# First two feed-forward pairs side by side, all their operands through DRAM

## The chip, the cores and the metric

The kernel runs on one core of one Trainium2 chip. A core has a matrix engine (TensorE, PE in the profile; PEld is its weight load), a vector engine (VectorE, DVE), a scalar engine (ScalarE, ACT), a slower general engine (GpSimd, POOL) and a queue engine that here only issues DMA transfers (SyncE, SP). Each runs its own instructions in the order in which they were written, and they meet through semaphores. The metric is device time of one execution in microseconds (us); lower is better.

## What is computed

One encoder block in fp32 on 1024 tokens of width 1024, 8 heads, feed-forward width 2816:

```python
h = modulate(layer_norm(x), sh1, sc1)
q, k, v, u, gates = split(h @ w_in)
a_out = diff_attention(q, k, v, lam, slopes, sub_g)     # 8 heads, two softmax maps each
p_out = multiscale_pool(u, w_pool, pool_scale)
ga, gp = split(gates)
mixed = sigmoid(ga) * a_out + sigmoid(gp) * p_out
x = layer_norm(ALPHA * x + g1 * (mixed @ w_out))
h = modulate(layer_norm(x), sh2, sc2)
gt, up = split(h @ w_ffn_in)
x = layer_norm(ALPHA * x + g2 * ((silu(gt) * up) @ w_ffn_out))
```

## The kernel before, in words

**Number format.** Each fp32 operand of a matrix product is split into a high and a low part (`split`, L97: ACT casts the high part, L98, and DVE or POOL subtracts it, L99). A product is three matmuls, high by high, high by low, low by high (`mm3`, L101 to L104). A `prod` is twelve matmuls of 128x512, four slices by three.

**Heads.** The eight heads run one after another, each in eight query blocks j. A table `fill` says which other work is written behind which block: projections for the next head, the normalisation and mixing of a finished half (`rms_mix`), and in head 7 the preparation of the out-projection's weights (`wo_prep`). The functions of `fill` are written by hand; within a head the order on each engine is set by a scheduler, and the buffers by pools in which a tag has `bufs` slots. A tile waits for its slot until the last reader of the slot's tile before it is done. Raw weights of 512 KB all come into tag `raw` with three slots: the eight raw slices `wor0` to `wor7` of the out-projection, and the raw feed-forward columns `eg` (gate) and `eu` (up).

**Out-projection.** `wo_prep(k)` loads slice k, ACT casts `wo_h`, POOL subtracts `wo_l`. `out_mm(t)` multiplies token tile t: two halves of eight slices of three matmuls into PSUM `y`. Tiles 0 and 1 are done by `early` at the end of head 7. They need all eight slices, and also `mx_0h`, the mixed first half of head 7, which is made behind the row factor `rm_0f` (six small POOL operations, L684 to L690).

**Feed-forward.** It runs in 22 pairs f of 128 gate and 128 up columns, over the second half of the tokens first, by a scheme with seven instead of eight block products (Strassen and Winograd). `first_mm(f)` makes two of the products from the gate columns; five more follow with operands called 0 to 4, which are sums and differences of the weight blocks, against five token operands `t2`, `t1`, `t3`, `b22`, `t4`. The token operands are made at the transition by short DVE and ACT functions: X and X2 subtract, X2h and X2l split `t2`; D3, D3h, D3l make `t3`; B22h, B22l `b22`; X3 and X3s `t4`. `M(t)` scales token tile t on ACT out of PSUM (L465).

**Prepared ahead.** In heads 6 and 7 the generator `ffn_units` splits weights and stores them in DRAM, one unit per query block: eight gate units for pairs 0 to 3 into `wgD`, and five operand units for pair 0 into `opD`. `first_w` and `first_op` load them on POOL's queue. Operands of pairs 1 to 21 are made on the spot during the pair before (POOL `ws` L1286 and L1326, DVE L1306 and L1318, splits by `operand`).

From the transition on (`manual_schedule`) the order of all engines is the order in which the code is written.

Of the kernel before, what the change touches and what calls it, by code (L numbers as in the profile page):

```python
# [9 lines left out]
F32 = mybir.dt.float32  # L10
# [25 lines left out]
def encoder_block_kernel(  # L36
# [447 lines left out]
    with ExitStack() as ctx2:  # L484
# [231 lines left out]
        def ffn_units():  # L716


            nxt = {}
# [20 lines left out]
            yield from halves_of(0, rg)  # L740
            r11, r12, r21, r22 = block(rg, 0), block(rg, 1), block(ru, 0), block(ru, 1)
            unit(opD[4], r22, "ou4")
            yield
            pol(r22, r21, r22, op=ALU.add)
            unit(opD[1], r22, "ou1")
            yield
            pol(r21, r11, r21, op=ALU.subtract)
            unit(opD[2], r21, "ou2")
            yield
            pol(r11, r22, r11, op=ALU.subtract)  # L750
            unit(opD[0], r11, "ou0")
            yield
            pol(r12, r12, r11, op=ALU.subtract)
            unit(opD[3], r12, "ou3")
            yield

# [97 lines left out]
        for h in range(NH):  # L854
# [18 lines left out]
            else:  # L873
# [27 lines left out]
            for j in range(8):  # L901
# [57 lines left out]

    def first_w(f):  # L960
        w = (wp.tile([P, KT, P], F32R, tag="whi", bufs=2, name="wg%d_h" % f),
             wp.tile([P, KT, P], F32R, tag="wlo", bufs=2, name="wg%d_l" % f))
        for a in range(2):
            nc.gpsimd.dma_start(w[a].rearrange("p a b -> p (a b)").bitcast(F32),
                                wgD[f, a].rearrange("p h c -> p (h c)"))
        return w

    def first_op(n):

        o = (fp.tile([P, 4, P], F32R, tag="oh", bufs=4, name="oh0_%d" % n),  # L970
             fp.tile([P, 4, P], F32R, tag="ol", bufs=4, name="ol0_%d" % n))
        for a in range(2):
            nc.gpsimd.dma_start(o[a].rearrange("p a b -> p (a b)").bitcast(F32), opD[n, a])
        ops_.setdefault(0, []).append(o)

# [58 lines left out]
    def X3s(t):  # L1034
        split(*cut(t4, t), f4_[t])

    f4_ = {}
# [58 lines left out]
    with tc.manual_schedule(engines={nc.vector.engine, nc.gpsimd.engine, nc.tensor.engine, nc.scalar.engine}):  # L1096
# [4 lines left out]
        R(5); S1(5); H(2); A(5); S2(5); N(5); H(3)  # L1101
        w_[0] = first_w(0)
# [4 lines left out]
        w_[1] = first_w(1)  # L1107
        y_[7] = out_mm(7, mt[7])
# [22 lines left out]
        th_tile = lambda nm: fp.tile([P, HF], F32, tag="th", bufs=4, name=nm)  # L1131
        X2h(6)
        D3l(5); X2l(4); X2l(5); X2l(6)
        first_mm(2, w_[2])
        w_[3] = first_w(3)
        first_op(0)
        D3(7); X(7); X2(7)
        X2h(7); D3h(6); B22h(7); D3h(7)
        first_cp(2)
        X2l(7)  # L1140
        first_op(1)
        for t in range(4, 8):
            split(*cut(t1, t), hr[:, 0:4, tcol(t)])
        first_add(2, False)
        first_op(2)
        first_mm(3, w_[3])
        D3l(6); D3l(7); B22l(7)
        first_cp(3)
        first_op(3)
        X3(4); X3(5)  # L1150
# [124 lines left out]
    with tc.manual_schedule(engines={nc.vector.engine, nc.gpsimd.engine, nc.tensor.engine, nc.scalar.engine,  # L1275
                                     nc.sync.engine}):
        load_pair(1)
        load_up(1)
        for f in range(NF):
            n = f + 1  # L1280
# [6 lines left out]
            if f == 0:  # L1287
                first_op(4)
# [4 lines left out]
            if f > 0:  # L1293
                operand(f, blocks(f)[3])
            half_mul(f, 0)
            if f >= BR:
                fw_step()
            if f > 0:
                a, c11, bc = chain[f]
                c = (ps_s("fc%d" % f) if bc is None else bc)[:, HF:]  # L1300
                prod(a, ops_[f][0], t2, False, False)
                u2 = ev_tile("u2_%d" % f)
                nc.scalar.copy(u2, a)
            load_pair(f + 2)
# [3 lines left out]
            fw_store()  # L1308
            if f > 0:
                fw_step()  # L1310
            if f > 0:
                prod(c, ops_[f][1], t1, True, False)
                p5 = ev_tile("p5_%d" % f)
                nc.scalar.copy(p5, c)
            else:
                a, _, c, u2, p5 = chain[f]
            if more:
# [24 lines left out]
            fw_store()  # L1342
            fw_step()
            if f == NF - 1:
                fw_store()
                out_ops = first_out()
            half_out(f, 0, a)
            fw_store()
            if f == 0:
                hrs.close()  # L1350
                fwp = hp.enter_context(tc.tile_pool(name="fwp", bufs=1, side="right", reuse_waits="tile"))
                prep = fw_prep()
                next(prep)
    hp.close()
# [249 lines left out]
```

## Time and profile before

| what | value |
|---|---|
| three runs | 1614.96, 1617.89, 1618.81 us; median 1617.89 |
| profiled execution | 1616.56 us, of which the span from the first to the last instruction 1614.8 |
| TensorE busy | 1558.5 us, 97% of the span |
| mean granted TensorE clock | 0.991 of full speed |
| VectorE, ScalarE, GpSimd busy | 72%, 44%, 21% |

The times of a trace row are microseconds from the span's start; what the execution takes outside its span is 1.8 us. TensorE is nearly always busy, so the time can only change where TensorE waits, where its clock is lowered, or where work on it is added or removed.

### The profile page before, as it was taken

How to read it: one execution, taken by the hardware profiler on the slowest of the kernel's cores; microseconds unless marked ns; L12 is line 12 of the kernel's file. 1: busy time of each engine (PE TensorE's matmuls, PEld its weight loads, DVE VectorE, ACT ScalarE, POOL GpSimd, SP SyncE). 2: the span in 40 equal slices, each digit the busy share in tenths (PEclk: the TensorE clock that was granted, in tenths of full speed). 3: DMA queues.
4: the chain of work that ended last, by engine and by line, in shares of the span. 5: the costliest groups of instructions: out<-in, count | busy, mean ns of one | idle time of the engine just before them, and what ended most of it. 6: DMA issues, size and time to landing. Idle time of an engine off the chain costs nothing. (4 is left out here: it accounts for less than half of the span.)

```text
span 1614.8 us, 20838 instructions
## 1 busy us (share of the span) xinstructions
PE 1558.5 (97%) x7634; PEld 1299.6 (80%) x7634; DVE 1161.7 (72%) x1706; ACT 706.2 (44%) x1228; POOL 338.4 (21%) x363
## 2 busy tenths in 40 slices
PE   6899999999999999999998998999999999999996
PEld 3787888888888888888887876888888888788885
DVE  8675869597786758677674888877877888336487
ACT  4445545455454545455561244444444444323220
POOL 4300001010001211101042232433333433100013
PEclk9999999999999999999999999999999999999999
DMA  9244415142431533243526554766666665996673
GB/s 332 63 114 143 141 60 150 59 135 75 114 115 52 157 111 98 78 144 119 170 72 192 175 187 145 258 220 212 233 228 235 208 228 183 373 388 212 201 274 127
DMA packets 191448, 273.90 MB, mean 170 GB/s; under 512 B 10161, under 2 KB 126962, under 8 KB 191346
## 3 DMA queue, kind: packets, MB, share of 16 engines
q1 hardware_dynamic: 183984, 251.04, 47.1%
q0 software_dynamic: 4400, 16.25, 2.7%
q10 hardware_dynamic: 2962, 5.27, 1.0%
q8 instruction: 60, 0.98, 0.3%
q14 instruction: 42, 0.34, 0.1%
HBM read 180.26 MB, written 83.89 MB: 164 GB/s over the span
## 5 line engine op out<-in xcount | busy, mean ns | idle before, releaser
L640 ACT ACTIVATE e<-e,nm 128x1024 f32<-128x1024 f32 x128 | 147.1, 1151 | 108.4 <-DVE nm L638 107.1
L638 DVE CUSTOM_DVE_ANT_0 e<-s,table 128x1024 f32<-128x1024 f32 x128 | 153.1, 1217 | 21.7 <-PE s L633 21.2
L631 PE MATMUL s<-k,q 128*128 128x512 f32 x256 | 105.2, 411 | 1.2 <-DVE nm L638 1.2
L99 DVE TENSOR_TENSOR al<-at,ah 128x512 fp32r<-128x512 f32 x128 | 83.2, 684 | 29.1 <-ACT ah L98 28.5
L633 PE MATMUL s<-k,q 128*128 128x512 f32 x256 | 101.6, 397 | 0.0
L645 DVE SCALAR_TENSOR_TENSOR e<-e,c,e 128x1024 f32<-128x1024 f32 x64 | 87.3, 1364 | 1.8
L98 ACT CAST oh<-ws 128x512 fp32r<-128x512 f32 x84 | 51.7, 616 | 83.3 <-POOL ws L1326 45.2
L98 ACT CAST ah<-at 128x512 fp32r<-128x512 f32 x128 | 70.0, 596 | 40.5 <-PE at L654 40.5
L99 DVE TENSOR_TENSOR ol<-ws,oh 128x512 fp32r<-128x512 f32 x84 | 70.4, 839 | 19.0 <-ACT oh L98 18.9
L99 DVE TENSOR_TENSOR fw<-fw,fw 128x512 fp32r<-128x512 f32 x77 | 80.1, 1040 | 0.0
L1326 POOL TENSOR_TENSOR ws<-rg,ru 128x512 f32<-128x512 f32 x21 | 44.4, 2112 | 152.2 <-DVE ol L99 152.2
L654 PE MATMUL at<-ident,e 128*128 128x128 f32 x512 | 68.9, 275 | 5.5 <-DVE e L645 3.2
L102 PE MATMUL av<-ah,vh 128*128 128x256 f32 x256 | 73.8, 288 | 0.3 <-ACT ah L98 0.2
L104 PE MATMUL av<-ah,vl 128*128 128x256 f32 x256 | 72.5, 283 | 0.0
L103 PE MATMUL av<-al,vh 128*128 128x256 f32 x256 | 72.4, 283 | 0.0
L104 PE MATMUL oa<-w,mol 128*128 128x512 f32 x176 | 68.6, 390 | 1.2 <-DVE mol L99 1.2
L102 PE MATMUL oa<-w,moh 128*128 128x512 f32 x176 | 68.6, 390 | 0.0
L103 PE MATMUL oa<-w,moh 128*128 128x512 f32 x176 | 68.5, 389 | 0.0
L102 PE MATMUL fa<-oA,oh 128*128 128x512 f32 x176 | 68.5, 389 | 0.0
L103 PE MATMUL fa<-oA,oh 128*128 128x512 f32 x176 | 68.5, 389 | 0.0
L104 PE MATMUL fa<-oA,ol 128*128 128x512 f32 x176 | 68.5, 389 | 0.0
L654 PEld LDWEIGHTS at<-ident,e 128*128 128x128 f32 x512 | 58.8, 144 | 11.2 <-DVE e L645 3.6
(578 smaller groups left out, 4608.1 us busy)
## 6 DMA issues: line engine op xcount, KB each, us to landing
wfD<-fw SPq DMA_DIRECT2D x77, 512.0 KB, 3.5
w<-wfD SPq DMA_DIRECT2D x77, 512.0 KB, 4.3
ada<-in_w_ada_dram SPq DMA_DIRECT2D x32, 512.0 KB, 3.8
fw<-in_w_ffn_out_dram SPq DMA_DIRECT2D x44, 256.0 KB, 4.4
rg<-in_w_ffn_in_dram SPq DMA_DIRECT2D x21, 512.0 KB, 4.2
ru<-in_w_ffn_in_dram SPq DMA_DIRECT2D x21, 512.0 KB, 3.8
midD<-th SPq DMA_DIRECT2D x42, 256.0 KB, 2.2
q<-q SPq DMA_DIRECT2D x32, 256.0 KB, 2.9
```

The source lines that it names most:

```text
L98: nc.scalar.copy(hi, src)
L99: (eng or nc.vector).tensor_tensor(lo, src, hi.bitcast(F32), op=ALU.subtract)
L102: nc.tensor.matmul(ps, lh, rh, start=start, stop=False, skip_group_check=skip)
L103: nc.tensor.matmul(ps, lh, rl, start=False, stop=False, skip_group_check=skip)
L104: nc.tensor.matmul(ps, ll, rh, start=False, stop=stop, skip_group_check=skip)
L631: nc.tensor.matmul(ps[:, cs], q[:, 0, jj * P:(jj + 1) * P], kd[h, m][:, cs], start=True, stop=False)
L633: nc.tensor.matmul(ps[:, cs], q[:, 1, jj * P:(jj + 1) * P], kd[h, m][:, cs], start=False, stop=True)
L638: nc.vector.tensor_tensor_reduce(out=t, in0=ps, in1=table[:, o0:o0 + S], scale=-slope, scalar=3.0e38, op0=ALU.add, op1=ALU.min, accum_out=nm)
L640: nc.scalar.activation(t, t, AF.Exp, bias=nm, scale=-1.0, accum_out=zt[:, m, j:j + 1])
L645: nc.vector.scalar_tensor_tensor(s[1], s[1], c1, s[0], op0=ALU.mult, op1=ALU.add)
L654: nc.tensor.matmul(pt[:, i, :], a[:, kt * P:(kt + 1) * P], ident, start=True, stop=True, is_transpose=True)
L1326: pol(sa, blocks(n)[0], blocks(n)[2], op=ALU.subtract)
```

## The change

All seven products' operands of pair 1 are made in the attention phase too, as those of pair 0 were. The gate units move from heads 6 and 7 to heads 4 and 5, and the ten operand units run in head 7 (one or two per query block, from j = 1). For pair 1 this brings two raw loads (`eg1`, `eu1`), five splits and four POOL additions or subtractions (L741 to L750 after) into head 7. In head 7 the second part of the mixing of the first half moves one place up. At the transition `first_w(2)` and `first_w(3)` are issued on ACT's queue, ahead of `M(7)`; X2h(6) goes ahead of `M(7)`; `t1` is made earlier and D3h(6), D3h(7) and B22h(7) later. The products of pairs 0 and 1 are written out alternately, and pair 2's operands are made during them. The arithmetic is the same.

```diff
-    opD = dram.tile([5, 2, P, HF], F32, tag="opD", name="opD")
+    opD = dram.tile([2, 5, 2, P, HF], F32, tag="opD", name="opD")
...
-                t = at.tile([P, 2, HF], F32R, tag="acc", name=nm)
+                t = at.tile([P, 2, HF], F32R, tag="mh" if nm[0] == "w" or nm[-1] in "13" else "acc", name=nm)
...
-            for f in (1, 2, 3):
+            for f in (3, 2, 1, 0):
                 yield from halves_of(f, gcols(f))
-            rg, ru = gcols(0), load_raw(wcols(wfi, DFF), "eu0")
...
+            for f in (0, 1):
+                rg, ru = gcols(f), load_raw(wcols(wfi, DFF + f * P), "eu%d" % f)
+                r11, r12, r21, r22 = block(rg, 0), block(rg, 1), block(ru, 0), block(ru, 1)
+                unit(opD[f, 4], r22, "ou%d_4" % f)
+                pol(r22, r21, r22, op=ALU.add)
+                yield
+                unit(opD[f, 1], r22, "ou%d_1" % f)
+                pol(r21, r11, r21, op=ALU.subtract)
+                yield
+                unit(opD[f, 2], r21, "ou%d_2" % f)
+                pol(r11, r22, r11, op=ALU.subtract)
+                yield
+                unit(opD[f, 0], r11, "ou%d_0" % f)
+                pol(r12, r12, r11, op=ALU.subtract)
+                yield
+                unit(opD[f, 3], r12, "ou%d_3" % f)
+                yield
...
-                    6: [lambda: wo_prep(4), lambda: wo_prep(5), lambda: wo_prep(6), lambda: wo_prep(7)],
-                    7: [lambda: rms_mix(h, 0, 1), lambda: early(0), lambda: early(1)],
+                    6: [lambda: wo_prep(4), lambda: wo_prep(5), lambda: wo_prep(6), lambda: wo_prep(7),
+                        lambda: rms_mix(h, 0, 1)],
+                    7: [lambda: early(0), lambda: early(1)],
...
-                elif h >= 6 and (h, j) > (6, 0):
-                    next(units, None)
+                elif h in (4, 5) and j % 4 == 3:
+                    next(units)
+                    next(units)
+                elif last and j > 0:
+                    for _ in range(1 + (2 < j < 6)):
+                        next(units, None)
...
         first_add(0, False); N(7); T(7)
+        w_[2] = first_w(2, nc.scalar)
         first_cp(1)
+        w_[3] = first_w(3, nc.scalar)
...
-        X2h(5)
+        X2h(5); X2h(6)
         M(7)
-        w_[2] = first_w(2)
...
-        for f in range(NF):
+        half_gate(0, 0, chain[0][1])
+        for n in range(2):
+            first_op(1, n)
+        a, _, c, u2, p5 = chain[0]
+        prod(a, ops_[0][2], t3, False, False)
...
+        prod(c, ops_[0][3], b22, False, True)
...
+        rest_a(1)
...
+        prod(a1, ops_[1][2], t3, False, False)
...
+        prod(c1, ops_[1][3], b22, False, True)
...
+        pair_ops(2, 0)
+        prod(a, ops_[0][4], t4, False, True)
+        pair_ops(2, 1)
...
+        prod(a1, ops_[1][4], t4, False, True)
...
+        pair_ops(2, 3)
+        for f in range(2, NF):
```

`rest_a(f)` holds the two products with operands 0 and 1 (`t2`, `t1`). `pair_ops(2, step)` is new and makes pair 2's operands in four steps: step 0 is the POOL addition `ws`, a DVE subtraction and a split.

On POOL, at the end of head 7, before the change, from the last two operations of `rm_0f` on:

```order
L95 TENSOR_TENSOR rm_0f<-rm_0v,mhalf 128x4
L690 TENSOR_TENSOR rm_0f<-rm_0f,rm_0m 128x4
L99 TENSOR_TENSOR wo_l<-wor_7547,wo_h 128x1024
L99 TENSOR_TENSOR wo_l<-wor_7551,wo_h 128x1024
L99 TENSOR_TENSOR wo_l<-wor_7555,wo_h 128x1024
L682 TENSOR_TENSOR rm_1z<-zt_6952 128x4
L683 TENSOR_SCALAR rm_1v<-rm_1z 128x4
L686 TENSOR_SCALAR rm_1z<-rm_1z 128x4
L99 TENSOR_TENSOR wo_l<-wor_7559,wo_h 128x1024
```

The same place after it:

```order
L95 TENSOR_TENSOR rm_0f<-rm_0v,mhalf 128x4
L690 TENSOR_TENSOR rm_0f<-rm_0f,rm_0m 128x4
L741 TENSOR_TENSOR eu_7422<-eu_7422 128x512
L744 TENSOR_TENSOR eu_7422<-eg_7420,eu_7422 128x512
L747 TENSOR_TENSOR eg_7420<-eu_7422,eg_7420 128x512
L750 TENSOR_TENSOR eg_7420<-eg_7420 128x512
L99 TENSOR_TENSOR wo_l<-wor_7514,wo_h 128x1024
L682 TENSOR_TENSOR rm_1z<-zt_6962 128x4
L683 TENSOR_SCALAR rm_1v<-rm_1z 128x4
L686 TENSOR_SCALAR rm_1z<-rm_1z 128x4
L99 TENSOR_TENSOR wo_l<-wor_7518,wo_h 128x1024
L99 TENSOR_TENSOR wo_l<-wor_7568,wo_h 128x1024
```

Before, four of the eight `wo_l` stood ahead of these rows and four are left; after, two stand ahead, then come the four operations of pair 1 (`eu`, `eg`), and six `wo_l` are left.

On SP, in head 7, before the change (`wor` are the raw slices of the out-projection):

```order
L793 DMA wor_7502<-woD 128x1024
L793 DMA wor_7547<-woD 128x1024
L793 DMA wor_7551<-woD 128x1024
L793 DMA wor_7555<-woD 128x1024
L793 DMA wor_7559<-woD 128x1024
```

After it, the part from the second raw slice on:

```order
L791 DMA wor_7412<-woD 128x1024
L108 DMA eg_7420<-in_w_ffn_in_dram 128x8x128
L108 DMA eu_7422<-in_w_ffn_in_dram 128x8x128
L725 DMA opD<-ou_3_7416 128x2x512
L791 DMA wor_7514<-woD 128x1024
L725 DMA opD<-ou_4_7424 128x2x512
L725 DMA opD<-ou_1_7522 128x2x512
L791 DMA wor_7518<-woD 128x1024
L725 DMA opD<-ou_2_7527 128x2x512
L791 DMA wor_7568<-woD 128x1024
L798 DMA mt_0_7798<-mixD 128x7x128
L791 DMA wor_7572<-woD 128x1024
```

The raw columns of pair 1 now take slots of tag `raw` between the second and the third slice. `eg_7420` keeps its slot until the last operand unit is split, behind all slices, so that slices 2 to 7 go through two slots.

On ACT, at the transition, before the change (L1079 is X2h, L1067 B22h, the row of L465 is `M(7)`):

```order
L1079 CAST oA<-hr 128x4x128
L986 COPY p_1_8559<-fa_8521 128x512
L1067 CAST oB<-hr 128x4x128
L1079 CAST oA<-hr 128x4x128
L465 ACTIVATE hr<-m_7t,modc 128x128 x8
L1079 CAST oA<-hr 128x4x128
L1079 CAST oA<-t2s 128x4x128
```

After it (L1089 is X2h, L1077 B22h, L967 `first_w`):

```order
L1089 CAST oA<-hr 128x4x128
L967 DMA wg_h<-wgD 128x1024
L967 DMA wg_l<-wgD 128x1024
L989 COPY p_1_8593<-fa_8551 128x512
L967 DMA wg_h<-wgD 128x1024
L967 DMA wg_l<-wgD 128x1024
L1077 CAST oB<-hr 128x4x128
L1089 CAST oA<-hr 128x4x128 x2
L465 ACTIVATE hr<-m_7t,modc 128x128 x8
```

The two pairs of weight loads stand on ACT ahead of `M(7)`, and X2h of tile 6 stands ahead of it too.

## Rows read from the trace of the kernel before

**Rows 1.** The page: busy time of the engines, and one group of instructions.

```profile
PE 1558.5 (97%) x7634; PEld 1299.6 (80%) x7634; DVE 1161.7 (72%) x1706; ACT 706.2 (44%) x1228; POOL 338.4 (21%) x363
...
L645 DVE SCALAR_TENSOR_TENSOR e<-e,c,e 128x1024 f32<-128x1024 f32 x64 | 87.3, 1364 | 1.8
```

**Rows 2.** Waits of TensorE, 840 to 1045 us: total, times, longest.

```profile
PE fa L102 <- issue: 6.1, 1, 6.1
PE at L654 <- DVE e L645: 3.2, 1, 3.2
PE y L102 <- ACT mx_0h L98: 2.4, 1, 2.4
PE fa L102 <- DMA wg_h<-wgD: 2.0, 1, 2.0
...
PE fa L104 <- DMA wg_l<-wgD: 0.5, 1, 0.5
```

**Rows 3.** Timeline of TensorE, out-projection: start, duration.

```profile
876.94 0.48 PE L102 MATMUL y<-wo_h,mt 128*128 128x512 f32 x1
877.42 0.39 PE L102 MATMUL av<-ah,vh 128*128 128x256 f32 x1
...
881.63 0.28 PE L104 MATMUL av<-ah,vl 128*128 128x256 f32 x1
```

**Rows 4.** Timeline of POOL, end of head 7.

```profile
832.03 10.51 POOL L99 TENSOR_TENSOR wo_l<-wor,wo_h 128x1024 fp32r<-128x1024 f32 x4 [16.79 <-ACT wo_h L98]
842.50 0.20 POOL L684 TENSOR_TENSOR rm_0v<-rm_0s,rm_0v 128x4 f32<-128x4 f32 x1
...
844.60 8.05 POOL L99 TENSOR_TENSOR wo_l<-wor,wo_h 128x1024 fp32r<-128x1024 f32 x3
...
854.37 2.40 POOL L99 TENSOR_TENSOR wo_l<-wor,wo_h 128x1024 fp32r<-128x1024 f32 x1
```

**Rows 5.** The tile wor, all eight: duration ns min/median/max, and landing.

```profile
L98 ACT CAST wo_h<-wor x8: 1049/1052/1070, 830.9 to 850.4; 128x1024 fp32r<-128x1024 f32 x8
L99 POOL TENSOR_TENSOR wo_l<-wor,wo_h x8: 2348/2406/3408, 832.0 to 854.4; 128x1024 fp32r<-128x1024 f32 x8
...
DMA to landing us min/median/max: 3.2/3.4/6.8
```

**Rows 6.** DMA issues, 740 to 870 us: KB each, median us to landing.

```profile
eu<-in_w_ffn_in_dram SPq DMA_DIRECT2D x1, 512.0 KB, 4.2
```

**Rows 7.** POOL by form, 980 to 1500 us: busy us, mean ns.

```profile
L1326 POOL TENSOR_TENSOR ws<-rg,ru 128x512 f32<-128x512 f32 x21 | 44.4, 2112 | 152.2 <-DVE ol L99 152.2
L1286 POOL TENSOR_TENSOR ws<-ru 128x512 f32<-128x512 f32 x21 | 32.8, 1560 | 54.3 <-DMA ru<-in_w_ffn_in_dram 36.6 <-ACT u L1090 9.5 <-DVE th L1261 3.8
```

**Rows 8.** Timeline of TensorE, transition to the feed-forward.

```profile
969.53 0.47 PE L102 MATMUL fa<-h0h,wg_h 128*128 128x512 f32 x1 [2.02 <-DMA wg_h<-wgD]
...
981.29 0.39 PE L102 MATMUL fa<-oA,oh 128*128 128x512 f32 x1
981.52 0.39 PE L103 MATMUL fa<-oA,oh 128*128 128x512 f32 x1
...
998.75 0.76 PE L102 MATMUL fa<-oB,oh 128*128 128x512 f32 x1 [6.07 <-issue]
```

**Rows 9.** A stretch: busy us (instructions) by engine, granted clock, DMA share, GB/s.

```profile
1000.00:1020.00 20.00, 20.00 (x84) 16.35 (x84) 14.46 (x21) 9.26 (x17) 7.43 (x6) 0.93 0.64 207
```

**Rows 10.** Timeline of DVE: head 7, and the transition.

```profile
847.32 3.07 DVE L645 SCALAR_TENSOR_TENSOR e<-e,c,e 128x1024 f32<-128x1024 f32 x1
...
971.90 0.69 DVE L1076 TENSOR_TENSOR hr<-hr 128x512 f32<-128x512 f32 x1
...
997.97 0.68 DVE L1323 TENSOR_TENSOR p<-p,fa 128x512 f32<-128x512 f32 x1
```

**Rows 11.** Timeline of ACT, transition.

```profile
969.17 2.90 ACT L465 ACTIVATE hr<-m_7t,modc 128x128 f32<-128x128 f32 x8
972.63 0.62 ACT L1079 CAST oA<-hr 128x512 fp32r<-128x512 f32 x1 [0.56 <-DVE hr L1076]
```

More of the change, by code (lines that the diff above doesn't have):

```diff
@@ L963, in first_w, with first_op @@
         for a in range(2):
[L964 to L971 removed]
+            q.dma_start(w[a].rearrange("p a b -> p (a b)").bitcast(F32),
+                        wgD[f, a].rearrange("p h c -> p (h c)"))
+        return w
+    def first_op(f, n):
+        o = (fp.tile([P, 4, P], F32R, tag="oh", bufs=4, name="oh%d_%d" % (f, n)),
+             fp.tile([P, 4, P], F32R, tag="ol", bufs=4, name="ol%d_%d" % (f, n)))
         for a in range(2):
[L973 to L974 removed]
+            nc.gpsimd.dma_start(o[a].rearrange("p a b -> p (a b)").bitcast(F32), opD[f, n, a])
+        ops_.setdefault(f, []).append(o)
     def first_mm(f, w):
@@ L1035, in X3s, with T1l, T1 @@
         split(*cut(t4, t), f4_[t])
+    def T1l(t):
+        o = cut(t1, t)
+        vec(o[1], hr[:, 0:4, tcol(t)], o[0].bitcast(F32), op=ALU.subtract)
+    def T1(t):
+        split(*cut(t1, t), hr[:, 0:4, tcol(t)])
     f4_ = {}
@@ L1131, in encoder_block_kernel @@
         th_tile = lambda nm: fp.tile([P, HF], F32, tag="th", bufs=4, name=nm)
-        X2h(6)
         D3l(5); X2l(4); X2l(5); X2l(6)
         first_mm(2, w_[2])
-        w_[3] = first_w(3)
-        first_op(0)
+        first_op(0, 0)
         D3(7); X(7); X2(7)
-        X2h(7); D3h(6); B22h(7); D3h(7)
+        T1(4)
+        nc.scalar.copy(cut(t1, 5)[0], hr[:, 0:4, tcol(5)])
+        X2h(7); X2l(7)
+        first_op(0, 1)
+        nc.scalar.copy(cut(t1, 6)[0], hr[:, 0:4, tcol(6)])
+        nc.scalar.copy(cut(t1, 7)[0], hr[:, 0:4, tcol(7)])
         first_cp(2)
[L1140 to L1143, printed above, removed]
+        T1l(5)
         first_add(2, False)
-        first_op(2)
+        T1l(6); T1l(7)
+        D3h(6); B22h(7); D3h(7)
+        first_op(0, 2)
         first_mm(3, w_[3])
@@ L1148, in encoder_block_kernel @@
         first_cp(3)
-        first_op(3)
+        first_op(0, 3)
         X3(4); X3(5)
@@ L1276, in encoder_block_kernel, with pair_ops @@
                                      nc.sync.engine}):
-        load_pair(1)
-        load_up(1)
-        for f in range(NF):
+        load_pair(2)
+        load_up(2)
+        load_pair(3)
+        def pair_ops(n, step):
+            w11, w12, w21, w22 = blocks(n)
+            if step == 0:
+                ops_[n, "s"] = [evp.tile([P, 4, P], F32, tag="st", bufs=2, name="ws%d_%d" % (n, i)) for i in range(2)]
+            sa, sb = ops_[n, "s"]
+            if step == 0:
+                pol(sa, w21, w22, op=ALU.add)
+                vec(sb, sa, w11, op=ALU.subtract)
+                operand(n, sb)
+            elif step == 1:
+                vec(sb, w12, sb, op=ALU.subtract)
+                operand(n, sa)
+                pol(sa, w11, w21, op=ALU.subtract)
+            elif step == 2:
+                operand(n, sa)
+            else:
+                operand(n, sb)
+        half_gate(0, 0, chain[0][1])
[3 more added lines that the diff above has]
+        prod(a, ops_[0][2], t3, False, False)
+        vec(p5, p5, a, op=ALU.add)
+        half_mul(0, 0)
+        first_op(1, 2)
+        prod(c, ops_[0][3], b22, False, True)
+        vec(u2, u2, c, op=ALU.add)
+        half_gate(0, 1, u2)
+        first_op(1, 3)
+        rest_a(1)
+        hrs.close()
+        fwp = hp.enter_context(tc.tile_pool(name="fwp", bufs=1, side="right", reuse_waits="tile"))
+        prep = fw_prep()
+        next(prep)
+        first_op(0, 4)
+        a1, _, c1, u21, p51 = chain[1]
+        first_op(1, 4)
+        prod(a1, ops_[1][2], t3, False, False)
+        half_mul(0, 1)
+        vec(p51, p51, a1, op=ALU.add)
+        half_out(0, 1, p5)
+        prod(c1, ops_[1][3], b22, False, True)
+        vec(u21, u21, c1, op=ALU.add)
+        half_gate(1, 0, chain[1][1])
+        half_mul(1, 0)
+        pair_ops(2, 0)
+        prod(a, ops_[0][4], t4, False, True)
+        pair_ops(2, 1)
+        half_gate(1, 1, u21)
+        pair_ops(2, 2)
+        load_up(3)
+        half_out(0, 0, a)
+        prod(a1, ops_[1][4], t4, False, True)
+        half_mul(1, 1)
+        half_out(1, 1, p51)
+        half_out(1, 0, a1)
+        pair_ops(2, 3)
+        for f in range(2, NF):
             n = f + 1
@@ L1292, in encoder_block_kernel @@
             half_gate(f, 0, chain[f][1])
-            if f > 0:
-                operand(f, blocks(f)[3])
+            operand(f, blocks(f)[3])
             half_mul(f, 0)
-            if f >= BR:
+            if f > 2:
                 fw_step()
[L1298 to L1303, printed above, removed]
+            a, c11, bc = chain[f]
+            c = (ps_s("fc%d" % f) if bc is None else bc)[:, HF:]
+            prod(a, ops_[f][0], t2, False, False)
+            u2 = ev_tile("u2_%d" % f)
+            nc.scalar.copy(u2, a)
             load_pair(f + 2)
@@ L1308, in encoder_block_kernel @@
             fw_store()
[L1309 to L1316, printed above, removed]
+            fw_step()
+            prod(c, ops_[f][1], t1, True, False)
+            p5 = ev_tile("p5_%d" % f)
+            nc.scalar.copy(p5, c)
             if more:
@@ L1343, in encoder_block_kernel @@
             fw_step()
+            if f == 3:
+                fw_step()
             if f == NF - 1:
@@ L1348, in encoder_block_kernel @@
             fw_store()
[L1349 to L1353, printed above, removed]
     hp.close()
```

25 lines of the change are left out of this document (3 added, 22 removed).

## The prediction

> **What bounds the kernel now.** I read the page first: TensorE is busy 97% of the span, VectorE 72% and ScalarE 44% [rows 1]. So only TensorE's own idle time and its clock can be won or lost. Next the waits of TensorE, limited to the two places that the change touches. Five matter there [rows 2]. At the end of head 7 it waits 3.2 us for the softmax tile `e` and 2.4 us for `mx_0h`. At the transition it waits 2.0 and 0.5 us for the weights of `first_mm(2)`, and 6.1 us ahead of one matmul of a product. The profile calls the last one "issue", so I looked at VectorE's timeline beside it: the product starts at 998.75 [rows 8] just after the DVE addition `p<-p,fa`, which reads the PSUM tile that it overwrites, has ended at 997.97 + 0.68 = 998.65 [rows 10]. That addition is queued behind the splits of `t4` and those of pair 1's operands. The reader should see that this wait belongs to VectorE's backlog. Last, the clock: the stretch from 1000 us has 0.93 with TensorE fully busy [rows 9], so 14% of its 20 us, 2.8 us, went at the lower level, 1.2 instead of 2.4 GHz. With the part from 998.75 on that is 4.05 us in which half the work was done, a loss of 2.0 us.
>
> **Part one, the transition: a gain.** What can be won is 2.0 + 0.5 + 6.1 us of waits and 2.0 us of clock, 10.6 us. Step by step:
>
> Weights of pairs 2 and 3 are issued earlier, on a queue where nothing is waiting. `first_mm(2)` then starts at 969.53 - 2.02 = 967.5 [rows 8]. One matmul takes 0.227 us (981.29 to 981.52 [rows 8], rounded there), a `prod` of twelve 2.72. After three products, at 975.7, `first_mm(3)` needs the PSUM tile that `M(7)` empties. `M(7)` now stands behind X2h(6). Its source X2(6) ends at 971.90 + 0.69 = 972.59 [rows 10], the cast takes 0.62 and `M(7)` 2.90 [rows 11], so it ends at 976.2 where it ended at 972.07. The wait is 0.5 us. Behind `M(7)` stand X(7), X2(7), X2h(7) and X2l(7), in sum four DVE operations of 0.69 and one cast of 0.62: 3.4 us, with hand-overs near 4, so `t2` is whole at about 980.2. `first_mm(3)` is through at 978.9 and `rest_a(0)` starts at 980.2 instead of 981.29 [rows 8]. Of 2.5 us, 1.1 are won.
>
> The 6.1 us wait: four products (10.9 us) now stand between the product with `b22` and the one with `t4` of pair 0, and VectorE is rid of five splits and two subtractions of pair 1, 7 x 0.69 = 4.8 us. Either covers the backlog. I count the 6.1 and the 2.0 us of clock as won, 8.1.
>
> Pair 2's operands are the next that can be late. From `pair_ops(2, 0)` two products, 5.4 us, pass before the first is used; it needs a POOL addition (1.56 to 2.11 us, [rows 7]), two DVE operations (1.38) and a cast (0.62): 3.6 to 4.1 us with nothing in the way, but `half_gate`, `half_mul` and `half_out` of two pairs share DVE and ACT. If they fit, it costs 0.3; if four of those 0.69 us operations stand ahead it costs 2.9. I take 1.6. The operand loads of pair 1 cost nothing: eight products lie between the first issue and the last use. If that cover were gone, a late load would cost up to its landing.
>
> Gain of this part: 1.1 + 8.1 - 1.6 = 7.6 us, from 6.3 to 8.9.
>
> **Part two, the end of head 7: a loss.** Before, POOL made the eight `wo_l` between 832.03 and 856.77, only interrupted by `rm_0f` and three small operations [rows 4]; three raw slots let each load run under the subtractions. TensorE reached tile 2 at 876.94 [rows 3]. After the change four POOL operations and two loads stand between the second and third slice, and slices 2 to 7 use two slots, since `eg1` holds the third. The chain:
>
> 1. The first two `wo_l` at 10.51/4 = 2.63 us each: 832.0 + 5.3 = 837.3 [rows 4].
> 2. `eu1` takes the slot that the second leaves, 4.2 us [rows 6]: 841.5.
> 3. ACT casts it (0.62) ahead of the copy that `rm_0f` needs, together 0.8: 842.3. Then `rm_0f`, 844.60 - 842.50 = 2.1 [rows 4]: 844.4. TensorE waits here for `mx_0f`, which moved up.
> 4. Four POOL operations of 128x512. The rows have means of 1.56 and 2.11 [rows 7]; I take the middle, 1.84, as both rows have the same shape: 7.4, 851.8. The third `wo_l` 2.63: 854.4.
> 5. The fourth slice's load waits for the third's slot, the sixth's for the fourth's and the eighth's for the sixth's. Each round is a load 3.4, a cast 1.05 [rows 5], `wo_l` 2.63 and 0.1 between: 7.2. Three rounds: 876.0.
> 6. In the order, 52 matmuls of tiles 0 and 1 stand behind the first that needs the eighth `wo_l`: 11.8 us. Tile 2 starts at 887.8, 10.9 later than before.
> 7. Before, the 24 `av` matmuls of the last block (0.12 us each, 2.9) and the `ms` and transposes about them (1.2) ran after the start of tile 2 [rows 3]; now they run in the waits. That gives back 4.1. The longer waits bring one more stretch of lowered clock, priced as the one above, 2.0 at most; I take 1.8.
>
> Loss: 10.9 - 4.1 + 1.8 = 8.6 us. Lower bound: POOL operations of 1.56, loads of 3.2, `wo_l` of 2.35 [rows 5] and no clock loss: rounds of 6.7, the eighth ends at 873.1, loss 3.9. Upper bound: 2.11, one load of 6.8 [rows 5]: 880.5, loss 13.1.
>
> A row shows POOL and VectorE in each other's way: while `wo_l` ran, L645 took 3.07 us [rows 10], where its group's mean is 1.36 [rows 1]. The Trainium skill has a rule for it ("SBUF — State Buffer", section "SBUF: two separate sides"): the port pair that GpSimd and VectorE share is an exclusive lock, so that a VectorE operation with two SBUF inputs waits until a GpSimd operation that holds it is done. By that rule four more POOL operations block VectorE up to four times; the row agrees. What this makes of the time is the fourth rival.
>
> **The rest.** The gate units in heads 4 and 5 add eight pairs of a cast (0.62) and a DVE split (0.69) there and take them out of heads 6 and 7. VectorE and ScalarE have room [rows 1]; with no cover they would cost 10.5 us, but then their leaving heads 6 and 7 would win as much. I count 0, as I do for `t1` and D3h, B22h, which only change places within the cover of `first_mm`.
>
> **Sum.** 1616.56 (the profiled execution, span 1614.8) + 8.6 - 7.6 = 1617.6. The three runs have a median 1.3 above that execution, so the median forecast is 1618.9, put down as 1619: no change that can be told. A measurement of this kernel can tell about 0.3%, 4.9 us. Its own range goes from 3.9 - 8.9 = -5.0 to 13.1 - 6.3 = +6.8: 1613 to 1625.
>
> **Rivals.**
> 1. *Slower: loads on the two slots decide.* Rounds in step 5 run beside the `mt` loads and `opD` stores that now stand between them on SP. If two of the three loads take the longest landing, 6.8 [rows 5], the sum rises by 6.8: 1626. For it: SP issues in order, and a slice's load stands behind stores that wait for splits. Against it: 3.4 is the median of eight. It decides once the eighth `wo_l` ends after about 880.
> 2. *Faster: the chain is covered.* If the eighth `wo_l` ended by 869 (rounds of 5 us, or loads that come earlier), tile 2 would start near 881, its 4.1 us are given back, and the loss is about 0 to 1: 1618 - 7 = 1611. For it: TensorE has `av`, transposes and the first slices of two tiles to do in between. Against it: a round's three durations alone are 7.1.
> 3. *The change doesn't do what it says.* If pair 2's operands or `M(7)` give back most of the transition, the gain is 3 instead of 7.6: 1623.5. For it: the operand chain has under 2 us to spare.
> 4. *VectorE is blocked in head 7.* Four POOL operations of 1.84 keep it from the splits and `e` tiles that `at` and `mx_0h` wait for; half of their 7.4 us would reach TensorE: 1622.7. Against it: TensorE is waiting for `wo_l` there anyway.
>
> **Chances.** My forecast 0.50, the rivals 0.20, 0.17, 0.06 and 0.07. Faster by over 0.3%: rival 2 and a little of the forecast's lower end, 0.19. Slower: rival 1, half of 3 and 4, and the upper end of the forecast, 0.31. Within: 0.50. The range that leaves out no more than 2 in 10 reaches from rival 2's value to just beyond rival 1's: 1611 to 1627; outside stay loads slower still, and a chain wholly covered.
>
> **What the profile will show.** Right: no wait of over 1 us at the product with `t4` of pair 0, tile 2 starting near 888, the eighth `wo_l` ending near 876, waits of TensorE on POOL's `rm_0f` and `wo_l` in head 7. Wrong: if the `wo_l` end before 869 or the loads land in far over 3.4; if `rest_a(0)` starts later than 981 relative to `m_7t`; or if TensorE waits over 3 us for pair 2's operands.

## The result, and the profile after

The changed kernel takes 1626.81 us (median of four runs, 1626.48 to 1627.85) against 1616.91 for the kernel before on the same chip: a ratio of 1.0062, 95% interval 1.0045 to 1.008. It is slower by 10 us, 0.6%, which is clear of noise. The time lies within the range that was given, near its upper end. It lies 1.8 us above the forecast's own range (1613 to 1625), and the likeliest case, no change, was not what came.

The waits of TensorE after the change, from 840 to 1060 us and from 1060 us on (total, times, longest), answer to [rows 2]. They are quoted from two answers of the same view.

```profile
PE mx_0f L190 <- POOL rm_0f L690: 5.2, 1, 5.2
PE y L103 <- POOL wo_l L99: 4.0, 4, 1.3
PE fc L102 <- ACT p L1383: 3.3, 2, 2.7
PE fa L102 <- ACT p L989: 2.5, 1, 2.5
PE y L102 <- ACT wo_h L98: 1.7, 2, 0.9
PE fa L104 <- DMA wg_l<-wgD: 1.1, 1, 1.1
...
PE ob L102 <- DMA w<-wfD: 3.8, 1, 3.8
```

Of the five waits that the prediction started from, four are gone or at most 0.5 us. The fifth, on `wg_l`, grew from 0.5 to 1.1 us. Six others stand beside it, and only the first, the second and the fifth row are those of head 7 that were foreseen. The two rows `fc` and `fa ... p` are in pairs 2 to 4, and the last one is where the output stage begins, 350 us later.

To see what each is worth I took the starts of the same matmuls from the timelines of both traces. Two rows of the changed kernel and two of the kernel before stand for the method:

```profile
961.00 0.30 PE L460 MATMUL m_6t<-ident,m_6n 128*128 128x128 f32 x1
...
1013.98 0.39 PE L102 MATMUL fa<-oA,oh 128*128 128x512 f32 x1
```

```profile
954.51 0.30 PE L460 MATMUL m_6t<-ident,m_6n 128*128 128x128 f32 x1
...
1017.02 0.39 PE L102 MATMUL fa<-oA,oh 128*128 128x512 f32 x1
```

At `m_6t` the changed kernel is 6.5 us behind; at the first product of pair 2 it is 3.0 us ahead; and it ends 9.9 behind. The stages between such marks, in us:

| from | to | before | after | difference |
|---|---|---|---|---|
| first `wo_l` | `m_6t` | 122.48 | 129.24 | +6.8 |
| `m_6t` | pair 0, product with `t2` | 26.78 | 25.15 | -1.6 |
| there | pair 2, first product | 35.73 | 27.84 | -7.9 |
| there | pair 4, first product | 27.77 | 32.75 | +5.0 |
| there | pair 5, first product | 19.04 | 21.89 | +2.9 |
| there | pair 21, first product | 304.64 | 305.03 | +0.4 |
| there | end | 246.34 | 251.05 | +4.7 |

With the first `wo_l` 0.3 us earlier (831.76 against 832.03) the sum is +10.0, the difference of the spans is 1624.7 - 1614.8 = 9.9.

POOL's timeline at the end of head 7, after the change, answers to [rows 4]:

```profile
831.76 5.23 POOL L99 TENSOR_TENSOR wo_l<-wor,wo_h 128x1024 fp32r<-128x1024 f32 x2 [16.79 <-ACT wo_h L98]
...
844.51 1.26 POOL L741 TENSOR_TENSOR eu<-eu 128x512 f32<-128x512 f32 x1
...
850.17 2.41 POOL L99 TENSOR_TENSOR wo_l<-wor,wo_h 128x1024 fp32r<-128x1024 f32 x1
...
857.73 2.37 POOL L99 TENSOR_TENSOR wo_l<-wor,wo_h 128x1024 fp32r<-128x1024 f32 x1 [3.92 <-ACT wo_h L98]
...
864.95 2.46 POOL L99 TENSOR_TENSOR wo_l<-wor,wo_h 128x1024 fp32r<-128x1024 f32 x1 [1.53 <-ACT wo_h L98]
...
873.62 2.35 POOL L99 TENSOR_TENSOR wo_l<-wor,wo_h 128x1024 fp32r<-128x1024 f32 x1 [3.46 <-ACT wo_h L98]
```

From the first to the last `wo_l` it takes 44.2 us where it took 24.7. The reader should see POOL idle ahead of the last slices: it waits for the cast, the cast for the load, and the load for the slot.

### The profile page after: what moved, and what is told of

Read it like the earlier page. It is cut to its first block, busy times and chain, and to the rows that moved or that the text cites. A ratio compares the mean times of both kernels' runs of the same rounds, so it can differ in the third digit from the quotient of the medians.

```text
span 1624.7 us, 20878 instructions
## 1 busy us (share of the span) xinstructions
PE 1560.1 (96%) x7634; PEld 1300.8 (80%) x7634; DVE 1162.2 (72%) x1704; ACT 704.2 (43%) x1228; POOL 341.0 (21%) x371
```

## The experiments

Each kernel is compared with the kernel before in runs on the same chip. The changed kernel's ratio is 1.0062. Profiles of kernels with the same code up to there differ in when the first `wo_l` starts (831.76 in the changed kernel, 833.81 in the first experiment), so stages are compared from mark to mark.

Stages of the same code differ between profiles too, and a difference has to be larger than that. The changed kernel and those of experiments 1, 3 and 4 have the same code up to `m_6t`: their eight `wo_l` take 44.2, 46.0, 46.5 and 45.5 us, and `m_6t` comes 129.2, 130.2, 130.2 and 129.4 us after the first. Experiments 2, 5, 6 and 11 have the changed kernel's code from `m_6t` on: from pair 2 to pair 4 they take 31.2, 32.7, 31.2 and 31.6 us, and for the last stage 249.8, 249.2, 249.7 and 249.3, where the changed kernel takes 32.75 and 251.05.

**1. Head 7 alone.** The attention phase of the changed kernel with everything from `first_w` on of the kernel before:

```diff
-            nc.gpsimd.dma_start(o[a].rearrange("p a b -> p (a b)").bitcast(F32), opD[n, a])
+            nc.gpsimd.dma_start(o[a].rearrange("p a b -> p (a b)").bitcast(F32), opD[0, n, a])
```

> The attention phase of the changed kernel (gate units in heads 4 and 5, ten operand units in head 7, mixing moved up) with the transition and the feed-forward of the kernel before; pair 1's operands are stored and not used, the result is the same. Theory A (the chain through POOL and two raw slots in head 7 costs 6 to 7 us by itself, whatever follows): eighth wo_l ends near 876, m_6t starts 6.5 us later than before, total 6 to 7 us above the kernel before, about 1623. Rival B (what head 7 loses is covered again by the 6.1 us wait ahead of the t4 product, since VectorE works off its backlog in the meantime): the t4 wait shrinks and the total is within 2 us of the kernel before, about 1618.

Measured: 1625.54 us, ratio 1.0051 (1.0037 to 1.0064); the medians alone, against 1615.54, give 1.0062. From the first `wo_l` to `m_6t` 130.22 us, 7.7 more than before; the stages behind pair 2's first product are those of the kernel before to 0.02 us. From `m_7t` to the product with `t2` it takes 1.5 us longer. The waits for the weights are as before (1.9 and 0.5 us), but eight matmuls behind them take over 0.6 us instead of 0.39, the lower clock level (the granted clock from 978 to 985 us is 0.76). The wait ahead of the `t4` product is shorter (5.0 us instead of 6.1), and that stage with its clock takes 1.9 us less. Theory A holds: these two nearly cancel, and the loss of head 7 is not covered again.

**2. The units spread over heads 6 and 7.**

```diff
-                elif last and j > 0:
-                    for _ in range(1 + (2 < j < 6)):
-                        next(units, None)
+                elif h >= 6 and (h, j) > (6, 0):
+                    next(units, None)
```

> The changed kernel with its ten operand units spread one per query block over heads 6 and 7 (seven in head 6, three at the start of head 7), so that both raw loads and the four POOL operations of pair 1 are done before the first wo_l. Theory A: the eighth wo_l ends near 857 again, TensorE's waits on rm_0f and wo_l in head 7 (9 us) fall to those of the kernel before, m_6t starts 6 to 7 us earlier than in the changed kernel, total about 1620. Rival B (the late waits on operands and weights in the feed-forward set the time, and an earlier start only makes them longer): total 1625 to 1627. Rival C (the units cost as much in head 6): m_6t moves by under 3 us.

Measured: 1619.47 us, ratio 1.0021 (1.0013 to 1.003), so 0.41% is won back. The eight `wo_l` take 25.6 us, and from the first to `m_6t` it is 120.97 us, 8.3 less than in the changed kernel (6 to 7 expected) and 1.5 less than before the change. Theory A holds, though not in the wait on `rm_0f`: it is still 5.2 us, yet costs nothing that `m_6t` shows. What stays above the kernel before is the loss behind pair 2 (31.15 and 23.48 us instead of 27.77 and 19.04) and in the last stage (249.84).

**3. Pair 2's operands earlier.**

```diff
+        pair_ops(2, 0)
         vec(u21, u21, c1, op=ALU.add)
+        pair_ops(2, 1)
         half_gate(1, 0, chain[1][1])
         half_mul(1, 0)
-        pair_ops(2, 0)
         prod(a, ops_[0][4], t4, False, True)
-        pair_ops(2, 1)
```

> The changed kernel with pair 2's operand steps 0 and 1 written ahead of the half gates of pair 1, so that POOL's second addition is done some 2 to 3 us earlier and the raw slot for pair 3's up columns comes free earlier. Theory A (the 2.7 us wait ahead of pair 2's b22 product, with a stretch of lowered clock behind it, comes from the load of pair 3's up columns being issued late): the load is issued near 1012 instead of 1014.8, the wait goes, total 3 to 5 us below the changed kernel, about 1623. Rival B (that wait is VectorE's backlog of gate halves): the wait stays at 2 us or more, total within 1.5 us of the changed kernel.

Measured: 1622.14 us, ratio 1.0038 (1.0023 to 1.0052). The load of `ru` of pair 3 is issued 1.0 us ahead of pair 2's first product instead of 0.8 behind it, 1.8 us earlier. The wait ahead of pair 2's `b22` product, from TensorE's timeline of this kernel:

```profile
1025.33 0.50 PE L102 MATMUL fc<-oB,oh 128*128 128x512 f32 x1 [0.94 <-ACT p L1383]
```

In the changed kernel it was 2.73 us, so it fell by 1.8 too, with the load. From pair 2 to pair 4 it takes 29.40 us instead of 32.75. Theory A holds; the load moved less than I had expected, and 0.9 us stays. In the total it is less sure: the interval overlaps that of the changed kernel, and 1.6 us of the gain lie in the last stage (249.4 us), where the code is the same.

**4. The preparation steps.** `fw_step` prepares one of the 77 output weight tiles and `fw_store` issues its store.

```diff
+        fw_step()
         pair_ops(2, 2)
         load_up(3)
...
         half_out(1, 0, a1)
+        fw_store()
+        fw_step()
         pair_ops(2, 3)
+        fw_store()
...
-            if f == 3:
-                fw_step()
```

> The changed kernel with the two extra steps of the output weights' preparation put into the part where pairs 0 and 1 run side by side, and none extra in pair 3, so that all 77 are done by the end of pair 20 as before. Theory A (the 77th step falling into the last pair delays the last store and with it the first loads of the output stage; the second step in pair 3 makes ACT wait for a store): the 3.8 us wait on the weights at the start of the output stage goes down to under 1, the 2.5 us wait at the start of pair 4 goes, total 5 to 8 us below the changed kernel, about 1620. Rival B (the wait at the output stage comes from the last halves' stores, not from the weights' steps): it stays, total 2 to 3 us below.

Measured: 1620.24 us, ratio 1.0026 (1.0016 to 1.0035). From pair 4 to pair 5 it is 19.04 us again and the last stage 246.05, both as before the change. The first loads of the output stage are issued on SP in the changed kernel (`w<-wfD`), behind the last stores (`wfD<-fw`):

```profile
1376.13 0.38 SPq L1217 DMA_DIRECT2D wfD<-fw  x1
...
1377.93 6.75 SPq L1217 DMA_DIRECT2D wfD<-fw  x2
1384.81 1.18 SPq L1181 DMA_DIRECT2D w<-wfD  x2
```

and in this one, which is 1.6 us earlier at pair 21:

```profile
1376.26 0.39 SPq L1217 DMA_DIRECT2D wfD<-fw  x1
1377.46 1.05 SPq L1181 DMA_DIRECT2D w<-wfD  x2
```

One store fewer stands ahead. The loads go out 7.4 us earlier, 5.8 counted from pair 21. Theory A holds. The wait of pair 2 on `p` grows to 3.8 us (33.20 us from pair 2 to pair 4). I put this down to the two steps, which now run on ACT and DVE there; experiment 12 bears it out.

**5. The slots.** The last four units at block 5:

```diff
-                elif last and j > 0:
-                    for _ in range(1 + (2 < j < 6)):
+                elif last and 0 < j < 6:
+                    for _ in range((0, 1, 1, 2, 2, 4)[j]):
```

> The changed kernel with only the count of units per block in head 7 altered: the last four operand units of pair 1 run at block 5 instead of 5 to 7, so that pair 1's raw gate columns give back their slot before the sixth slice and the later slices use three slots. The four POOL operations stay. Theory A1 (two slots make most of the loss: three round trips of about 7 us): the eighth wo_l ends 4 to 7 us earlier than in the changed kernel, counted from the first, total 3 to 5 us lower, about 1623. Theory A2 (the POOL operations make it): it ends within 2 us of the changed kernel, total 1625 to 1627.

Measured: 1625.53 us, ratio 1.0057 (1.0041 to 1.0073), not told apart from the changed kernel. The last three `wo_l` now run back to back, but the eight take 42.0 us, 2.2 less than in the changed kernel and no more than the spread of 44.2 to 46.5. A1 alone, with 4 to 7, is wrong. The fourth slice's load still waits here until the third `wo_l` ends, so not every round trip is gone.

**6. Without POOL's operations for pair 1.**

```diff
-                pol(r22, r21, r22, op=ALU.add)
+                if f == 0:
+                    pol(r22, r21, r22, op=ALU.add)
```

and so for the other three.

> The changed kernel without the four POOL additions and subtractions of pair 1; so pair 1's operands 0 to 3 hold plain blocks and pair 1's products are not those of the reference. Loads, casts, splits, stores and slots are the same. Theory A2 (POOL's extra 5.7 us are passed on whole): the eighth wo_l ends 5 to 6 us earlier, total 4 to 6 us lower than the changed kernel, about 1622. Theory A1 (the slot round trips set the end): under 3 us earlier in the chain, total 0 to 3 us lower.

Measured: 1622.84 us, ratio 1.0042 (1.0028 to 1.0057). The eight `wo_l` take 42.2 us, 2.0 less, and to `m_6t` it is 128.39, 0.9 less than in the changed kernel, both about the spread. So A2, with 5 to 6 us, is wrong too in the chain. The total's interval overlaps that of the changed kernel. Where the profile is shorter, it is so in later stages: from pair 2 to pair 5 52.1 us instead of 54.6, and the last 249.66 instead of 251.05. The code there is the same, and why they differ stays open.

**7. The three corrections together** (experiments 2, 3 and 4 in one).

> The changed kernel with the three corrections together: operand units spread over heads 6 and 7, pair 2's operand steps earlier, the two preparation steps moved ahead of pair 2. Theory A (the three losses are separate): the differences to the changed kernel add up, 7 + 4.7 + 6.6 us, total about 1609, 6 to 8 us below the kernel before, which is what the transition wins. Rival B (what one correction wins runs into the next late operand): total 1613 to 1617, no better than the kernel before.

Measured: 1610.63 us (1607.76 to 1611.78), ratio 0.9967 (0.9955 to 0.9979): faster than the kernel before by 5.4 us. The three gains in ratio, 0.41%, 0.24% and 0.36%, sum to 1.01%; together they are 0.95%. Theory A holds, though 5.4 us is a little under the 6 to 8 expected. Its waits from 600 us on:

```profile
PE mx_0f L190 <- POOL rm_0f L690: 5.2, 1, 5.2
PE fc L102 <- ACT p L1386: 1.8, 1, 1.8
PE fa L102 <- ACT u L1377: 1.5, 1, 1.5
```

**8. The mixing back at its old place**, on top of experiment 7.

```diff
-                        lambda: rms_mix(h, 0, 1)],
-                    7: [lambda: early(0), lambda: early(1)],
+                    7: [lambda: rms_mix(h, 0, 1), lambda: early(0), lambda: early(1)],
```

> As the kernel with the three corrections, and the second part of head 7's mixing back at its old place. Theory A (TensorE's wait of 5.2 us on rm_0f in head 7 stands there because its four matmuls were moved up; back at the old place the same work fills it): that wait goes, those on e and mx_0h of the kernel before (3.2 and 2.4 us) come back, total within 1 us of the kernel with the three corrections. Rival B (moving it up costs by itself): total 2 to 4 us lower.

Measured: 1611.61 us, ratio 0.9972 (0.9962 to 0.9983), not told apart from experiment 7. The 5.2 us wait is replaced by 3.2 on `e` and 0.8 on `mx_0h`. From the first `wo_l` to `m_6t` it is 121.62 instead of 120.67: Theory A holds.

**9 and 10. The weights of pairs 2 and 3 on POOL's queue at their old places**, on top of experiment 7; in experiment 10 also X2h(6) behind `M(7)`.

```diff
         M(7)
+        w_[2] = first_w(2, nc.gpsimd)
...
-        X2h(5); X2h(6)
+        X2h(5)
         M(7)
+        X2h(6)
```

> The kernel with the three corrections, with the weights of pairs 2 and 3 loaded on POOL's queue at their old places behind M(7) again. Theory A (the early load on ACT wins the 2.5 us waits of first_mm(2), of which 1 to 2 us reach the end): TensorE waits about 2 us again on the weights, total 1 to 2.5 us above the kernel with the three corrections, about 1612. Rival B (the next waits, for t2 and for pair 2's operands, take it over): within 1 us.

> The kernel with the three corrections, with both the old places of those weight loads and X2h of tile 6 behind M(7) again. Theory A (putting X2h ahead of M(7) costs 0.5 us at PSUM and about 1 us at t2): 0.5 to 1.5 us below the kernel with only the old loads, M(7) ending 0.6 us earlier. Rival B (its place does nothing, since the weights come later than M(7) ends): no difference to it.

Measured: 1611.11 us (ratio 0.9969, 0.9957 to 0.998) and 1611.78 (0.9974, 0.9963 to 0.9984). In both TensorE waits 1.9 us for the weights again, and from `m_7t` to the product with `t2` it takes 14.73 and 14.75 us instead of 13.33; to pair 2's first product it is then 27.20 instead of 27.93. So 1.4 us are lost and 0.7 come back, which the totals can't tell from nothing (Rival B of experiment 9). X2h's place alone changes nothing here (Rival B of experiment 10).

**11. Experiments 5 and 6 together.**

> The changed kernel without pair 1's four POOL operations and with its last four units at block 5, so that the slot comes back early; pair 1's operands 0 to 3 hold plain blocks, so its products are not those of the reference. Theory A3 (POOL's operations and the slots cover each other: each alone hides behind the other): from the first to the last wo_l it takes 36 us or less where the changed kernel takes 44.2, and the total is near 1619. Rival B (the load of pair 1's up columns ahead of the row factor, and the order on ACT and SP that the units bring, set the chain): it takes 40 us or more, total 1622 to 1625.

Measured: 1623.34 us, ratio 1.0042 (1.0027 to 1.0056), which again overlaps the changed kernel's; the profiled execution took 1618.77 us. The eight `wo_l` take 39.4 us, 4.8 less than in the changed kernel (6 to 7 less than in the three others of its code), and `m_6t` is 3.9 us earlier where the parts gave 1.0 and 0.9. That hints that each partly hid behind the other; the spread of 1.0 us leaves it unsure. But 14.7 us of the 19.5 that the change added stay. The rows of POOL show where, and below them one of ACT and one of SP:

```profile
832.36 5.22 POOL L99 TENSOR_TENSOR wo_l<-wor,wo_h 128x1024 fp32r<-128x1024 f32 x2 [16.79 <-ACT wo_h L98]
846.59 2.39 POOL L99 TENSOR_TENSOR wo_l<-wor,wo_h 128x1024 fp32r<-128x1024 f32 x1 [1.42 <-ACT wo_h L98]
855.68 6.75 POOL L99 TENSOR_TENSOR wo_l<-wor,wo_h 128x1024 fp32r<-128x1024 f32 x2 [2.89 <-ACT wo_h L98]
864.69 7.09 POOL L99 TENSOR_TENSOR wo_l<-wor,wo_h 128x1024 fp32r<-128x1024 f32 x3 [2.27 <-ACT wo_h L98]
```

```profile
841.81 0.62 ACT L98 CAST ou<-eu 128x512 fp32r<-128x512 f32 x1 [4.29 <-DMA eu<-in_w_ffn_in_dram]
```

```profile
849.01 0.33 SPq L795 DMA_DIRECT2D wor<-woD  x1
```

There are 9 us between the second and the third, and 6.7 to the fourth, each up to a cast on ACT. In the first gap ACT stands 4.29 us for the load of `eu1`, ahead of the copy that `rm_0f` needs, as steps 2 and 3 of the prediction had it. In the second the load of the fourth slice is issued at 849.01, just when the third `wo_l` ends (846.59 + 2.39 = 848.98), so this slice still waits for a slot: the units at block 5 free one only for later slices. Rival B is nearer. How those us divide between the load of `eu1`, the slots, ACT's order and SP's order I did not separate; that they come with the units in head 7 is what experiment 2 shows.

**12. The extra steps later.** Experiments 2 and 3, and the extra steps in pairs 8 and 14:

```diff
-            if f == 3:
+            if f in (8, 14):
                 fw_step()
```

> The units spread over heads 6 and 7 and pair 2's operand steps earlier, as in the kernel with the three corrections, but the two extra preparation steps put into pairs 8 and 14 instead of the part where pairs 0 and 1 run side by side. Theory A (the 3.3 us that pairs 2 and 3 still lose in the kernel with the three corrections come from the steps' casts and stores there, and later pairs have room): from pair 2 to pair 4 28 to 29.5 us instead of 31.1, nothing lost at pairs 8 and 14, total 2 to 3 us lower, about 1608. Rival B (an extra step costs a wait for a store of about 2.5 us wherever it stands): the two pairs lose up to 5 us, total 1610 to 1614.

Measured: 1610.84 us, ratio 0.9967 (0.9955 to 0.998), the same as experiment 7. From pair 2 to pair 4 it takes 29.42 us, 1.7 less and as Theory A had it; but the pairs behind the extra steps take 20.68 and 20.61 us instead of 19.04. Rival B holds in kind (1.6 us each instead of 2.5): an extra step costs about as much wherever it stands in the steady part.

## Why the prediction was right, and where it was not

**Head 7: right in mechanism and in its end, wrong in two sizes that cancelled.** The eighth `wo_l` was to end at 876.0; it ended at 873.62 + 2.35 = 875.97. The row factor `rm_0f` was to be done at 844.4, and POOL's first operation of pair 1 starts at 844.51. The loads of the fourth, sixth and eighth slice are issued as the third, fourth and sixth `wo_l` end (852.58, 860.10, 867.41), which is the chain of step 5:

```profile
852.61 0.33 SPq L791 DMA_DIRECT2D wor<-woD  x1
...
860.12 0.33 SPq L791 DMA_DIRECT2D wor<-woD  x1
...
867.44 0.33 SPq L791 DMA_DIRECT2D wor<-woD  x1
```

But POOL's four operations took 1.26 to 1.62 us where I took 1.84, and the loads were slower. The tile wor in the changed kernel, to [rows 5]:

```profile
DMA to landing us min/median/max: 3.7/4.6/6.1
```

The median was 3.4. Rounds of 7.5, 7.3 and 8.6 us (ends of the third, fourth, sixth and eighth `wo_l`: 852.6, 860.1, 867.4, 876.0) stood against 7.2. That the end came out to the hundredth is luck: in the three other profiles of the same code the eight took 1.3 to 2.3 us longer.

The lost time to `m_6t` is 6.8 instead of 8.6 us. Tile 2 starts at the 97th of the `y` matmuls, 12.5 us later than before, where 10.9 and 1.8 for the clock were forecast:

```profile
889.47 0.39 PE L102 MATMUL y<-wo_h,mt 128*128 128x512 f32 x1
```

From there to `m_6t` it takes 71.5 us instead of 77.6, so 6.0 us are given back where step 7 had 4.1: this is the term that was mis-sized. And the explanation was too simple. Without POOL's four operations, and with the slot freed for the last slices, only 4.8 of the 19.5 us go (experiments 5, 6 and 11). The rest belongs to the loads, casts and the slot of the fourth slice that come with the units in head 7; its parts stay open.

**Transition: right.** From `m_6t` to the product with `t2` 1.6 us were won (1.1 forecast), and the 6.1 us wait with its stretch of lowered clock is gone: 7.9 won, 8.1 forecast. Which of the two covers it, the four products between or the work that VectorE is rid of, no run separates. The wait of 0.5 us for `M(7)` does not stand in the changed kernel. The 1.1 us for `wg_l` of pair 3 stand one product ahead, and these I had not foreseen: that load is issued on ACT only at 973.23 and is waited for until 980.85. In experiments 2 and 4, where that row is missing, TensorE waits 0.5 and 0.6 us on `hr` of `M(7)`. In the total neither shows (experiment 10).

**Pair 2's operands: the term that failed.** I priced them at 1.6 us, 2.9 at most. From pair 2 to pair 5 7.9 us were lost. I had followed the chain to pair 2's own first product, which did start without a wait; what is late is the next link, pair 3's up columns. The rows of the changed kernel, SP, POOL and DVE:

```profile
1014.78 0.38 SPq L108 DMA_DIRECT2D ru<-in_w_ffn_in_dram  x1
```

```profile
1019.02 1.38 POOL L1361 TENSOR_TENSOR ws<-ru 128x512 f32<-128x512 f32 x1 [4.27 <-DVE th L1274]
1020.37 1.73 POOL L1225 TENSOR_TENSOR fw<-fw,fw 128x512 f32<-128x512 f32 x1
```

```profile
1019.17 1.78 DVE L99 TENSOR_TENSOR ol<-ru,oh 128x512 fp32r<-128x512 f32 x1
1020.88 1.77 DVE L1286 SCALAR_TENSOR_TENSOR th<-th,p 128x512 f32<-128x512 f32 x1
1022.57 0.68 DVE L1377 TENSOR_TENSOR ws<-ws,rg 128x512 f32<-128x512 f32 x1
```

The load is issued at 1014.78, only when pair 2's second POOL operation (1013.46 + 1.29) has released the slot; POOL's first addition for pair 3 starts 4.2 us later. Its row names DVE's `th`, but that ended 0.37 us before, where POOL's operation at 1013.46 follows its release by 0.08. In the kernel before the same addition is put down to the load itself, issued at 1015.51:

```profile
1019.46 1.52 POOL L1286 TENSOR_TENSOR ws<-ru 128x512 f32<-128x512 f32 x1 [2.72 <-DMA ru<-in_w_ffn_in_dram]
```

The subtraction on DVE follows at 1022.57, ACT's cast and its copy of `p` behind it, and the `b22` product starts at 1025.03. After the change and before it:

```profile
1025.03 0.50 PE L102 MATMUL fc<-oB,oh 128*128 128x512 f32 x1 [2.73 <-ACT p L1383]
```

```profile
1025.61 0.50 PE L102 MATMUL fc<-oB,oh 128*128 128x512 f32 x1 [0.27 <-ACT p L1314]
```

In the kernel before the same product waited only 0.27 us: it was the next limit already, and I had not looked at how far it stood behind the wait that I removed. From the issue of the load to this product it is 10.25 us in the changed kernel, 10.26 in experiment 3 and 10.10 before, so the product moves with the load. The stretch that follows has matmuls of 0.63 instead of 0.39 us, the lower clock level (the granted clock from 1020 to 1030 us is 0.83, before 1.00), 1.7 us over that product. So this place costs 2.73 + 1.7 + 0.56 at pair 3 - 0.27 = 4.7 of the 5.0 us up to pair 4. Experiment 3 takes 3.4 of the 5.0 us away; against the shortest profile of the same code (31.2 us from pair 2 to pair 4) it is 1.8.

The two DVE operations at 1019.17 and 1020.88 took 1.78 and 1.77 us where the same forms take 0.69, and each started while a POOL operation ran and ended some 0.55 us after it. The Trainium skill ("SBUF — State Buffer", section "SBUF: two separate sides") calls the port pair that the two engines share an exclusive lock, held for the whole instruction; the traces agree. It cost some 2.2 us in this chain, of which some 1.5 were there before the change (1.12 and 1.77 us for the same two). In head 7, where I had made it a rival, it shows as well (`ou` splits of 2.9 us). Experiment 6 takes the four added POOL operations out and gains 0.9 us to `m_6t`, about the spread, where that rival had 3.7; so alone they do not make it.

**The preparation steps: a term left out.** Pair 1 lost its three steps. Two of them went into pair 3, where two now stand together at the end, and the 77th falls into the last pair. ACT's rows of the changed kernel at pair 4:

```profile
1053.70 0.62 ACT L98 CAST fw<-fw 128x512 fp32r<-128x512 f32 x1 [3.83 <-issue]
1054.23 0.58 ACT L989 COPY p<-fa 128x512 f32<-128x512 f32 x1
```

The copy that TensorE waits for (2.53 us at 1054.86) stands behind the cast of such a step, which itself starts only after 3.83 us without work on ACT; what it waits for the profile does not name. This and the late load at the output stage cost 2.9 and 4.7 us, 7.6 in all, and experiment 4 takes both away. In other profiles of the same code the late load cost 2.9 to 3.5 us (last stage 249.2 to 249.8). The code shows the moved steps; I counted none of them.

**The sum and the chances.** The forecast sum was +8.6 - 7.6; with what was measured it is +6.8 - 9.5 + 7.9 + 0.4 + 4.7 - 0.3 = 10.0. Of the rivals the first gave 1626, nearly the time that came, but for a reason that did not hold: the longest landing was 6.1 us and the eighth slice was not late. The range reached to 1627 only because of this rival, so that the measured time lies in it is luck; what the forecast missed comes from two terms, pair 2's operands, priced too low, and the preparation steps, left out. Rival 3, that late operands give back the transition's gain, was right in kind, and I had given it 0.06. The units in heads 4 and 5 cost nothing that shows, as forecast: the first `wo_l` starts 0.3 us before its old time. Since it starts between 831.8 and 833.8 in profiles of the same code, a cost of up to some 2 us is not ruled out.

## What to carry to other kernels

Where a wait is removed, measure how far the next link of the same chain stands behind it (here 0.27 us of wait was already there), because a gain ends at the first operand that cannot come earlier. Count the small background steps that a rewritten loop hosts: one step short in a fixed budget came out as 3 to 4.7 us three hundred us later. And a change may hold a real gain under a loss that belongs only to where its extra work is put: spread over two heads instead of one, with two other corrections, the same idea is 0.33% faster than the kernel before.

## What the runs showed of the hardware that was not expected

The raw slices of 512 KB landed in 3.4 us (median) before, and in 4.6 us in the changed kernel, where stores and other loads stand among them on SP; that these lengthen it is not shown by a run of its own. The wait of 5.2 us on `rm_0f` cost nothing measurable between two marks (experiments 7 and 8): without it TensorE waits 3.2 us on `e` and 0.8 on `mx_0h` instead. The longest wait in a list is not the dearest.
